# Scaling the second branch's rows in the middle stages of a hybrid trunk kernel, and starting its output pairs in text order

## The chip, the core and the metric

The kernel runs on one core of a Trainium2 chip. A core has TensorE (matmuls, "PE" in the profile; its weight loads are "PEld"), VectorE ("DVE"), ScalarE ("ACT"), GpSimd ("POOL") and SyncE ("SP"), each with a queue of its own that is worked off in order, and 16 DMA engines that all queues share. The metric is the device time of one execution in microseconds; several executions are made, and the median is given.

## What is computed

One layer of a decoder trunk on a sequence of 1024 tokens with 1024 channels, float32. Two branches (HGRN2 and GLA, both gated linear attention) run on the same normalised input; each is normalised, gated, projected, and the two are merged by sigmoid gates:

```python
proj = h @ w_in[l]
hq, hf, hi, hz, gq, gk, gv, gz, ga, mg = jnp.split(proj, IN_OFFSETS, axis=-1)
y_h = hgrn2_branch(hq, hf, hi, hz, lb_all[l], hgrn_norm_w[l])
y_g = gla_branch(gq, gk, gv, gz, ga, gla_alpha_w[l], gla_alpha_b[l], gla_norm_w[l])
u_h = y_h @ w_branch[l, 0]
u_g = y_g @ w_branch[l, 1]
mg = jax.nn.sigmoid(mg.reshape(B, T, N_BRANCH, D_MODEL))
merged = mg[:, :, 0] * u_h + mg[:, :, 1] * u_g
x = x + gate[:, None, :] * (merged @ w_out[l])
return rms_norm(x, final_norm_w)
```

The part that matters here is the end of the HGRN2 branch. Its norm runs over all 1024 channels, so its factor for a token is known only when the last of its eight heads is done:

```python
o = rms_norm(o.reshape(B, T, HGRN_WIDTH), norm_w)
return o * jax.nn.silu(hz)
```

## The kernel before

**Tiles.** Work tiles come from a pool of 46 slots of 128 partitions x 1024 float32 (`Slots`). A slot that is freed goes to the end of a list, and the next request takes the one at its head; a tile may therefore have to wait for the last use of the tile that had the slot before. Every float32 matmul of size is made of three: operands are split into a high part (cast by ACT, L195, L1297, L1319) and a low part (the difference, by VectorE, L196, L1298, L1320), and high x high, high x low and low x high are added up.

**First part, up to about 816 us.** Projections of the input run as jobs of a `Stream`, one after another, their matmuls on L518, L577 to L579, L620 to L622. Between them `Stream.weave` puts small pieces of two tracks: `side`, the attention heads (generators that yield after each piece how many units of matmul work to wait for), and `back`, preparations such as sums of weights. One unit passes with each piece of a job. The products with the silu gate close each job (L929 on ACT, L930 on VectorE).

**Second part, `last_stages`, from about 816 us on.** Four stages b = 0 to 3 of 1024 x 1024 x 1024 products: the merge gates of the GLA and of the HGRN2 branch (b = 0, 1), then the projection of the GLA branch (b = 2) and of the HGRN2 branch (b = 3). Each is made with seven products of half size in place of eight, in the order `PRODUCTS = (1, 2, 5, 3, 6, 7, 4)`. Each product has four pairs i = 0 to 3; `Pair.run(p)` issues 12 matmuls of 128x128 by 128x512 (L1377), with one unit of weave after the sixth and one after the twelfth, so two units for a pair. So (0, 5, 3) is stage 0, product 5, pair 3. `Pair.after` takes sums and snapshots of the accumulators (L1349, L1351, L1364). The last head of HGRN2 still runs on the side track in stage 0; the other side work and the whole back track are through by then.

The left operands are prepared ahead in `prep_duo` (L1319 on ACT, L1320 on VectorE, one for two pairs). The right operands of stages 2 and 3 are the four quadrants of a branch's output. They are read from memory by `load_quad` (L1269), two tiles each, in the stage before; `combine` (L1280) takes differences of them and `build` (L1297, L1298) splits them.

**The factor.** After head 7 of HGRN2, `inverse_root` computes 1/rms for each token (L940 to L943) and the tile is kept in `rst_h` until stage 3 begins. `scale_quad` (L1276) multiplies the quadrants of `yh` with it when they have been loaded, at the end of stage 2. All of `yh` was stored by `put_act` (L893, POOL's queue).

**Queues and order.** Loads are issued on SP's queue, stores of intermediates on POOL's. Outside a first stretch with a fixed order, the order of the instructions on each engine is made when the kernel is built: a planner runs the program text on a model of the engines and lets an instruction that it takes to be ready go ahead of earlier ones on the same engine that it takes to be waiting. `tc.keep_in_program_order(m)` binds an instruction behind the one that stands before it on its engine in the text. Slots are handed out in text order, whatever the planner does.

**Accumulators.** Pairs 0 and 1 of (0, 1) share one tile of two banks, pairs 2 and 3 another. One of the two is free when stage 0 begins, the other is the one that the last job's product (L930) still reads.

Of the kernel before, what the change touches and what calls it, by code (L numbers as in the profile page):

```python
# [15 lines left out]
P = 128  # L16
# [66 lines left out]
def hybrid_trunk_kernel(  # L83
# [6 lines left out]
    nc = tc.nc  # L90
# [9 lines left out]
    S = Slots(sp, N_SLOTS)  # L100
# [71 lines left out]
    h_d, yg_d, yh_d = acts("h"), acts("yg"), acts("yh")  # L172
# [889 lines left out]
    def hgrn_attention(h):  # L1062
        st = h_state
        y = [None]
        sq = [None]

        def post(vh, half, po):
            if half == 0:
                y[0], sq[0] = st.pop(("z", h)), S.get([T])
            sl = slice(half * 512, half * 512 + 512)  # L1070
            nc.scalar.activation(sq[0][:, sl], po, AF.Square)
            nc.vector.scalar_tensor_tensor(y[0][:, sl], po, vec[:, R_HN + h:R_HN + h + 1],
                                           y[0][:, sl], ALU.mult, ALU.mult)

        yield from attention(st.pop(("q", h)), st.pop(("k", h)), st.pop(("f", h)), lambda: st[("v", h // 4)],
                             h % 4 * P, P, post)
        if h % 4 == 3:
            S.free(*st.pop(("v", h // 4)))
        put_act(yh_d, h, y[0])
        if ssq[0] is None:  # L1080
            ssq[0] = sq[0]
        else:
            nc.gpsimd.tensor_add(ssq[0], ssq[0], sq[0])
            S.free(sq[0])
        if h == 7:
            yield 2
            rst = S.get([T])
            inverse_root(rst, ssq[0], D)
            S.free(ssq[0])
            rst_h[0] = rst  # L1090

    def hgrn_v(h):
        def done(v):
# [174 lines left out]
        for kk in range(2):  # L1268
            nc.sync.dma_start(quads[b, z][kk], part_of(acts_of[b], int(z[0]) - 1, int(z[1]) - 1, kk))  # L1269

    def scale_quad(b, z):
        half = int(z[1]) - 1
        rst = rst_h[0][:, half * 512:half * 512 + 512].unsqueeze(1).to_broadcast([P, 2, 512])
        for t in quads[b, z]:
            v = t.rearrange("p (a t) -> p a t", a=2)
            nc.vector.tensor_mul(v, v, rst)  # L1276

    def combine(b, dst, x, y):
        for kk in range(2):
            nc.vector.tensor_sub(quads[b, dst][kk], quads[b, x][kk], quads[b, y][kk])  # L1280
# [60 lines left out]
    class Pair:  # L1341
# [25 lines left out]
        def run(self, p):  # L1367
            if p in (1, 5):
                self.bank[BANK[p]] = R.get()
            o = self.bank[BANK[p]]  # L1370
            hi, lo = (z[:, self.i % 2, :] for z in wt[self.b, p, self.i // 2])
            h = H[0 if self.b == 1 else self.b, p]
            for kt in range(4):
                h_hi, h_lo = (z[kt // 2][:, kt % 2, :] for z in h)
                sl = slice(kt * P, (kt + 1) * P)
                for n, (a, c) in enumerate(((hi, h_hi), (hi, h_lo), (lo, h_hi))):
                    nc.tensor.matmul(o, a[:, sl], c, start=(p in (1, 5) and kt == 0 and n == 0),  # L1377
                                     stop=(kt == 3 and n == 2), skip_group_check=True)
                if kt % 2:
                    stream.weave(1)  # L1380
            if self.i % 2:
                S.free(*wt.pop((self.b, p, self.i // 2)))
# [153 lines left out]
    for b in (2, 3):  # L1536
        for p, i, z in ((3, 3, "11"), (6, 1, "21"), (6, 3, "12"), (7, 2, "22")):
            after(b - 1, p, i, lambda b=b, z=z: load_quad(b, z))
            if b == 3:
                p, i = {(3, 3): (7, 2), (6, 1): (7, 3), (6, 3): (4, 2), (7, 2): (4, 3)}[p, i]  # L1540
                after(2, p, i, lambda z=z: scale_quad(3, z))
        after(b, 1, 2, lambda b=b: combine(b, "11", "12", "11"))
        after(b, 2, 2, lambda b=b: combine(b, "12", "12", "22"))

# [6 lines left out]
            combine(b, "21", "21", "22")  # L1551
            drop_quad(b, "22")
        after(b, 6, 2, last_of_all)
    after(3, 1, 0, lambda: S.free(rst_h[0]))

    def begin():
        fetch_factor(GROUPS[0])
# [47 lines left out]
```

## Time and profile before

| | |
|---|---|
| median of 3 runs | 1246.13 us (1244.64 to 1246.9) |
| profiled execution | 1243.66 us, of which span 1242.0 us |
| mean granted TensorE clock | 0.993 |
| bytes moved by DMA | 168.82 MB |

The times in the profile are those of one execution, from its first to its last instruction. A row of a timeline shows the start in us, the duration in us, the engine, the line of the kernel, the operation, what it writes and reads (tile names without their numbers; `b` is any tile of the 46 slots, `pd`, `pm` and `sc_ps` are accumulators), its shapes and, in brackets, the idle time of the engine before it and what ended it. A row of a table of windows shows for a stretch how long each engine was busy and with how many instructions, the granted clock, the share of time in which the DMA engines were busy and the GB/s that they moved.

### The profile page before, as it was taken

How to read it: one execution, taken by the hardware profiler on the slowest of the kernel's cores; microseconds unless marked ns; L12 is line 12 of the kernel's file. 1: busy time of each engine (PE TensorE's matmuls, PEld its weight loads, DVE VectorE, ACT ScalarE, POOL GpSimd, SP SyncE). 2: the span in 40 equal slices, each digit the busy share in tenths (PEclk: the TensorE clock that was granted, in tenths of full speed). 3: DMA queues.
4: the chain of work that ended last, by engine and by line, in shares of the span. 5: the costliest groups of instructions: out<-in, count | busy, mean ns of one | idle time of the engine just before them, and what ended most of it. 6: DMA issues, size and time to landing. Idle time of an engine off the chain costs nothing.

```text
span 1242.0 us, 20840 instructions
## 1 busy us (share of the span) xinstructions
PE 1202.8 (97%) x8627; PEld 996.6 (80%) x8627; DVE 759.9 (61%) x1225; ACT 535.3 (43%) x786; POOL 115.7 (9%) x201
## 2 busy tenths in 40 slices
PE   5999999999999999999999999999999999998997
PEld 3676889889798888788887878877888887787786
DVE  5635535584848466877774366785422758979443
ACT  5547643434434234334323324457643644454222
POOL 4100000202111121011110101011100000000000
PEclk9989999999999999999999999999999999999999
DMA  9714010744544267265251112244547456235202
GB/s 325 258 52 136 24 28 19 260 157 145 170 151 147 81 200 244 96 187 166 74 186 52 51 35 69 75 156 169 184 158 243 154 186 195 77 102 178 110 35 101
DMA packets 126928, 168.82 MB, mean 136 GB/s; under 512 B 7019, under 2 KB 97185, under 8 KB 126834
## 3 DMA queue, kind: packets, MB, share of 16 engines
q1 hardware_dynamic: 115234, 129.53, 33.4%
q0 software_dynamic: 11552, 37.97, 8.0%
q8 instruction: 67, 1.10, 0.4%
q14 instruction: 27, 0.22, 0.1%
q10 hardware_dynamic: 48, 0.01, 0.0%
HBM read 125.53 MB, written 41.94 MB: 135 GB/s over the span
## 4 chain that ended last, share of the span: by engine, by line
PE 59%; issue 23%; DVE 8%; DMA 4%; ACT 3%; POOL 2%; SPq 0%; POOLq 0%; DVEq 0%; ACTq 0%
PE pd L518 14%; PE pd L1377 9%; PE sc_ps L1377 5%; PE pm L1377 4%; PE pd L343 3%; PE pd L620 2%; PE pd L621 2%; PE pd L622 2%; PE sc_ps L343 1%; DVE b L196 1%; PE pm L825 1%; PE pd L1147 1%; PE pd L1148 1%; PE pd L1149 1%; DMA b<-yh 1%
## 5 line engine op out<-in xcount | busy, mean ns | idle before, releaser
L518 PE MATMUL pd<-b,b 128*128 128x512 f32 x1632 | 386.7, 393 | 0.0
L518 PEld LDWEIGHTS pd<-b,b 128*128 128x128 f32 x1632 | 302.4, 188 | 64.3 <-issue 0.7
L1377 PE MATMUL pd<-b,b 128*128 128x512 f32 x720 | 175.5, 395 | 3.0 <-DVE b L930 1.5
L1377 PEld LDWEIGHTS pd<-b,b 128*128 128x128 f32 x720 | 134.4, 189 | 35.7 <-DVE b L930 1.9
L196 DVE TENSOR_TENSOR b<-b,b 128x1024 fp32r<-128x1024 f32 (+2 forms) x99 | 102.5, 1045 | 92.0 <-ACT b L195 75.3
L195 ACT CAST b<-b 128x1024 fp32r<-128x1024 f32 (+2 forms) x99 | 86.7, 888 | 109.1 <-PE pd L518 16.9
L1320 DVE TENSOR_TENSOR b<-b,b 128x1024 fp32r<-128x1024 f32 x56 | 68.2, 1222 | 68.8 <-ACT b L1319 50.5
L1319 ACT CAST b<-b 128x1024 fp32r<-128x1024 f32 x56 | 58.4, 1050 | 65.3 <-PE pd L1377 19.1
L1377 PE MATMUL sc_ps<-b,b 128*128 128x512 f32 x324 | 79.0, 391 | 0.9 <-ACT scT L770 0.9
L1377 PE MATMUL pm<-b,b 128*128 128x512 f32 x300 | 72.7, 390 | 3.3 <-DVE b L1320 3.3
L577 PE MATMUL pd<-b,b 128*128 128x256 f32 x256 | 74.6, 291 | 0.0
L579 PE MATMUL pd<-b,b 128*128 128x256 f32 x256 | 72.5, 283 | 0.0
L578 PE MATMUL pd<-b,b 128*128 128x256 f32 x256 | 72.4, 283 | 0.0
L1377 PEld LDWEIGHTS sc_ps<-b,b 128*128 128x128 f32 x324 | 60.4, 188 | 14.2 <-ACT scT L770 1.4
L1377 PEld LDWEIGHTS pm<-b,b 128*128 128x128 f32 x300 | 56.6, 189 | 15.6 <-DVE b L1320 3.7
L343 PE MATMUL pd<-b,b 128*128 128x512 f32 x192 | 56.6, 431 | 4.8 <-DVE b L322 2.6
L1298 DVE TENSOR_TENSOR b<-b,b 128x1024 fp32r<-128x1024 f32 x36 | 45.1, 1262 | 18.1 <-ACT b L1297 10.3
L1235 POOL DMA_DIRECT2D ws<-b x64 | 34.6, 541 | 192.6 <-DVE b L1229 87.3
L620 PE MATMUL pd<-b,b 128*128 128x512 f32 x128 | 51.3, 401 | 0.0
L343 PEld LDWEIGHTS pd<-b,b 128*128 128x128 f32 x192 | 37.3, 203 | 17.2 <-issue 3.4
L712 ACT COPY xb<-b 128x512 f32<-128x512 f32 x48 | 29.4, 620 | 48.8 <-PE sc_ps L692 26.6
L621 PE MATMUL pd<-b,b 128*128 128x512 f32 x128 | 50.0, 390 | 0.0
(269 smaller groups left out, 2010.6 us busy)
## 6 DMA issues: line engine op xcount, KB each, us to landing
b<-in_w_in_dram SPq DMA_DIRECT2D x66, 512.0 KB, 4.1
ws<-b POOLq DMA_DIRECT2D x64, 256.0 KB, 3.4
b<-ws SPq DMA_DIRECT2D x32, 512.0 KB, 4.4
b<-in_x_dram SPq DMA_DIRECT2D x16, 512.0 KB, 5.6
b<-in_ada_w_dram SPq DMA_DIRECT2D x32, 256.0 KB, 6.5
b<-in_w_branch_dram SPq DMA_DIRECT2D x16, 512.0 KB, 4.4
b<-h SPq DMA_DIRECT2D x14, 512.0 KB, 4.0
b<-in_w_in_dram SPq DMA_DIRECT2D x24, 256.0 KB, 3.8
```

Source lines behind the costliest of these rows:

```text
L195: nc.scalar.copy(hi, src)
L196: nc.vector.tensor_sub(lo, src, hi.bitcast(F32))
L343: nc.tensor.matmul(accs[f], wg(a, d, f), b[d][:, half * 512:half * 512 + 512], start=(d == 0 and n == 0), stop=(d == KT - 1 and n == 2))
L518: nc.tensor.matmul(ps[0:w, th * 512:(th + 1) * 512], a[:, k, 0:w], b[:, th * 512:(th + 1) * 512], start=(k == 0 and n == 0), stop=(k == KT ...
L577: nc.tensor.matmul(o, lh, hi[:, k % 4, :], start=(k == 0), stop=False)
L578: nc.tensor.matmul(o, lh, lo[:, k % 4, :], start=False, stop=False)
L579: nc.tensor.matmul(o, ll, hi[:, k % 4, :], start=False, stop=(k == KT - 1))
L620: nc.tensor.matmul(o, lh, hi[:, k % 2, :], start=(k == 0), stop=False)
L621: nc.tensor.matmul(o, lh, lo[:, k % 2, :], start=False, stop=False)
L1319: nc.scalar.copy(hi, t)
L1320: nc.vector.tensor_sub(lo, t, hi.bitcast(F32))
L1377: nc.tensor.matmul(o, a[:, sl], c, start=(p in (1, 5) and kt == 0 and n == 0), stop=(kt == 3 and n == 2), skip_group_check=True)
```

## The change

Three edits. A generator `scale_rows` goes onto the back track when the factor has been computed: it loads each of the eight tiles of `yh`, multiplies it with the factor, and stores it back to where it came from. `scale_quad` and its four calls at the end of stage 2 are gone, and the factor's slot is freed when the eight tiles are done, not after (3, 1, 0). And the first matmul of each of the four pairs of (0, 1) is bound to its place in the text.

```diff
             inverse_root(rst, ssq[0], D)
             S.free(ssq[0])
             rst_h[0] = rst
+            stream.back.append([scale_rows(), 1])
+
+    def scale_rows():
+
+        for half in range(2):
+            rst = rst_h[0][:, half * 512:half * 512 + 512].unsqueeze(1).to_broadcast([P, 2, 512])
+            for i in range(4):
+                y = S.get([2, 512])
+                nc.sync.dma_start(y.rearrange("p a t -> p (a t)"), yh_d[half][i])
+                yield 4
+                nc.vector.tensor_mul(y, y, rst)
+                nc.gpsimd.dma_start(yh_d[half][i], y.rearrange("p a t -> p (a t)"))
+                S.free(y)
+                yield 2
+        S.free(rst_h[0])
...
-    def scale_quad(b, z):
-        half = int(z[1]) - 1
-        rst = rst_h[0][:, half * 512:half * 512 + 512].unsqueeze(1).to_broadcast([P, 2, 512])
-        for t in quads[b, z]:
-            v = t.rearrange("p (a t) -> p a t", a=2)
-            nc.vector.tensor_mul(v, v, rst)
...
-                    nc.tensor.matmul(o, a[:, sl], c, start=(p in (1, 5) and kt == 0 and n == 0),
-                                     stop=(kt == 3 and n == 2), skip_group_check=True)
+                    m = nc.tensor.matmul(o, a[:, sl], c, start=(p in (1, 5) and kt == 0 and n == 0),
+                                         stop=(kt == 3 and n == 2), skip_group_check=True)
+                    if (self.b, p, kt, n) == (0, 1, 0, 0):
+                        tc.keep_in_program_order(m)
...
-            if b == 3:
-                p, i = {(3, 3): (7, 2), (6, 1): (7, 3), (6, 3): (4, 2), (7, 2): (4, 3)}[p, i]
-                after(2, p, i, lambda z=z: scale_quad(3, z))
...
-    after(3, 1, 0, lambda: S.free(rst_h[0]))
```

## The prediction

> **What bounds the kernel now.** I read the page first, then TensorE's timeline from the start of the closing stages to their end, then VectorE's timeline and the table of windows over the same stretch, then the waits of single lines.
>
> ```profile
> span 1242.0 us, 20840 instructions
> PE 1202.8 (97%) x8627; PEld 996.6 (80%) x8627; DVE 759.9 (61%) x1225; ACT 535.3 (43%) x786; POOL 115.7 (9%) x201
> ...
> 900.00:1040.00 140.00, 140.00 (x619) 115.79 (x618) 1.00 0.57 182
> 1040.00:1100.00 60.00, 58.98 (x255) 46.93 (x254) 1.00 0.42 130
> 1132.00:1146.20 14.20, 10.50 (x37) 7.56 (x35) 0.88 0.42 146
> ```
>
> TensorE is busy for 97% of the span, so every change has to show up as fewer or more empty microseconds on TensorE. The last three rows are windows of the closing-stage matmuls (L1377) alone; the number in brackets is their count. From 900 to 1040 us, 619 of them take 140 us, 0.226 us each, with nothing lost. From 1040 to 1100 us only 255 fit in 60 us: 60 − 255 × 0.226 = 2.3 us lost. From 1132 to 1146.2 it is 14.2 − 37 × 0.226 = 5.8 us, less about 0.4 us for two matmuls of the output projection that stand between them: 5.4 us. These two places, and the opening of the closing stages at 816 to 850 us, are where time can be had.
>
> ```profile
> 870.00:900.00 30.00, 30.00 (x133) 24.40 (x132) 14.78 (x16) 19.12 (x25) 3.78 (x7) 1.00 0.57 178
> 900.00:930.00 30.00, 30.00 (x134) 24.70 (x133) 8.49 (x7) 11.99 (x18) 2.69 (x5) 1.00 0.48 158
> 1020.00:1050.00 30.00, 29.37 (x130) 24.03 (x129) 22.44 (x25) 10.18 (x12) 0.00 (x0) 1.00 0.67 211
> 1050.00:1080.00 30.00, 29.87 (x130) 23.74 (x129) 29.53 (x32) 14.29 (x16) 0.00 (x0) 1.00 0.39 119
> 1080.00:1110.00 30.00, 29.73 (x131) 24.02 (x130) 22.55 (x23) 15.21 (x18) 0.00 (x0) 1.00 0.28 87
> 1110.00:1140.00 30.00, 26.59 (x113) 21.08 (x113) 29.05 (x43) 16.85 (x23) 0.00 (x0) 0.98 0.33 107
> ```
>
> The columns are PE, PEld, DVE, ACT, POOL busy, the granted clock, the DMA engines' share, GB/s. VectorE is full from 1050 to 1080 us (29.53 of 30) and again from 1110 to 1140 (29.05); from 870 to 930 us it is half empty or emptier.
>
> **Part 1: eight multiplies leave the end of stage b = 2.**
>
> ```profile
> L1276 DVE TENSOR_TENSOR b<-b,b x8: 1212/1216/1224, 1020.6 to 1061.7; 128x1024 f32<-128x1024 f32 x8
>   DMA b<-yh: 7.5, 3
> ...
> 1041.38 1.22 DVE L1276 TENSOR_TENSOR b<-b,b 128x1024 f32<-128x1024 f32 x1 [0.99 <-DMA b<-yh]
> 1044.86 0.68 DVE L1364 TENSOR_TENSOR b<-pd,b 128x512 f32<-128x512 f32 x1
> ...
> 1045.69 3.00 PE L1377 MATMUL pd<-b,b 128*128 128x512 f32 x12 [0.63 <-DVE b L1364]
> 1088.10 0.93 PE L1377 MATMUL pd<-b,b 128*128 128x512 f32 x3 [0.27 <-ACT b L1319]
> ```
>
> The multiplies hold VectorE for 8 × 1.216 = 9.7 us, and three of them made the queue stand 7.5 us in all until their rows had landed. Right behind one such wait, TensorE waits for the sum of L1364 (0.63 us), and it goes on losing fractions until 1100 us. Without 17 us of work and waiting, VectorE's jam of 1050 to 1080 us is gone, and with it most of the 2.3 us. Bounds: a gain of 2.3 us at most, since no more is lost there; 0 at least, if the interleaving of the pairs at the start of b = 3 costs it anyway. I take three quarters, 1.7 us, because the largest piece hangs on VectorE by its own row. The quads' loads stay where they are, so no queue changes here.
>
> **Part 2: the same eight multiplies, with a load and a store each, enter the middle stages.** The generator starts with the last unit of pair (0, 5, 3) and yields 6 units for a row; a pair gives 2 units and takes 12 × 0.226 = 2.7 us. So a row comes every 3 pairs, 8.1 us, and eight rows take 65 us, from about 867 to 933 us. The factor is there in time:
>
> ```profile
> 870.93 1.06 ACT L943 ACTIVATE b<-b 128x1024 f32<-128x1024 f32 x1
> L893 POOL DMA_DIRECT2D yh<-b x16: 539/548/556, 489.4 to 862.6; - x16
> fx<-b POOLq DMA_DIRECT2D x8, 512.0 KB, 6.6
> b<-yh SPq DMA_DIRECT2D x8, 512.0 KB, 3.4
> L1269 SPq DMA_DIRECT2D b<-yh x8: 319/338/426, 1016.3 to 1046.7; - x8
> ```
>
> VectorE gets 8 × 1.22 us over 65 us, 15% more on a load of 49% (14.78 of 30) and then 28%. POOL gets 8 issues of 0.55 us, 4.4 us, and is nearly idle. SP gets 8 issues of 0.34 us. A row lands in 3.4 us, is scaled in 1.2 and stored in 6.6 (as f_x's 512 KB were), so a slot is out for some 12 us. The DMA engines move 8 × 2 × 512 KB = 8.4 MB more in 65 us, 129 GB/s, on top of 178 and 158 GB/s; the stretch of 1020 to 1050 us carried 211 at a share of 0.67, so the share goes up to about 0.9, and landings may take longer. All of this lies under TensorE as long as VectorE's preparations stay ahead of it. The tightest one is this:
>
> ```profile
> 885.52 1.22 DVE L1320 TENSOR_TENSOR b<-b,b 128x1024 fp32r<-128x1024 f32 x1
> ...
> 889.52 1.98 PE L1377 MATMUL pm<-b,b 128*128 128x512 f32 x8
> ...
> 904.41 1.23 DVE L1320 TENSOR_TENSOR b<-b,b 128x1024 fp32r<-128x1024 f32 x1 [5.58 <-DMA gate<-b]
> SPq L1312 <- DVE b L1320: 17.0, 2, 10.5
> ```
>
> The low part made at 885.52 is done at 886.74, and the third matmul of the group that begins at 889.52 reads it, at 889.97: 3.2 us to spare; the neighbours have more. A multiply before it costs 1.2 us of that, and TensorE notices nothing. One that stands in VectorE's queue for its row as long as the worst of L1276 (3 waits share 7.5 us, so about 3.5 us for the longest) costs 3.5 + 1.2 − 3.2 = 1.5 us. Behind the waiting multiply stand the L1320 splits and the sums of L1364, and for them wait TensorE and SP, whose next weight load needs the slot that L1320 frees. Bounds: 0, and the price of rival 1. I take 0.5 us, a third of one such hit. The row holds one slot of 46 and the factor's slot comes back two stages earlier; after (3, 1, 0) the slots follow one another as before.
>
> **Part 3: the four pairs of (0, 1) begin in text order.**
>
> ```profile
> 816.27 1.52 PE L1377 MATMUL pd<-b,b 128*128 128x512 f32 x6
> 817.72 1.31 PE L660 MATMUL sc_ps<-xb,b 128*32 128x80 f32 x64
> 818.96 1.65 PE L1377 MATMUL pd<-b,b 128*128 128x512 f32 x6
> 822.10 5.73 PE L1377 MATMUL pd<-b,b 128*128 128x512 f32 x24 [1.48 <-DVE b L930]
> ...
> 820.83 1.21 DVE L930 TENSOR_TENSOR b<-b,pd 128x1024 f32<-128x1024 f32 x1
> 821.55 0.59 ACT L1351 ACTIVATE b<-pd 128x512 f32<-128x512 f32 x1
> ```
>
> In the order that the planner made of the old kernel, pair 0 comes first (the two sixes), then four matmuls of pair 2, all of pair 1, the rest of pair 2, and pair 3. Pair 2 waits for the bank that L930 reads until 822.04: that is the 1.48 us. Text order puts pair 1 in front. But its first matmul waits, by the old program's semaphores, for the snapshot of pair 0 (L1351; both lie in one accumulator tile), which ends at 822.14. One wait takes the place of the other, 0.1 us later. Bounds: −1.6 us, if ACT's queue is planned otherwise and the snapshot comes at once; +2.7 us, one pair's time, if pair 2 then waits again. I take +0.2 us.
>
> **Sum.** −1.7 + 0.5 + 0.2 = −1.0 us. The profiled execution took 1243.66 us (span 1242.0 and 1.66 around it), so 1242.7; it lies 2.47 us below the median of 1246.13, so the median of the new kernel comes to 1245.1 us.
>
> **Rivals.** 1. *Slower: the row loads get stuck in SP's queue, and VectorE stands behind them.* SP is in order, and in this very stretch it stood 10.5 us for one slot (the last row of the fence on preparations). A row's load behind such a wait comes up to 10.5 us late; its multiply, planned for a row on time, then holds VectorE, and beyond the 3.2 us to spare TensorE loses up to 7.3 us. It decides from a delay of 3.2 us on. At half of that, 10.5/2 + 1.2 − 3.2 = 3.3, and twice over the eight rows, 6.6: with −1.7 and +0.2 that is +5.1, so 1251.2 us; in one place only, +1.8. For it: three of eight rows were late when loaded with less traffic. Against it: the planner places a multiply behind the load it knows of, and SP's wait was itself for an L1320.
>
> 2. *Much faster: the stall at the end goes too.*
>
> ```profile
> 1126.90 1.05 ACT L1319 CAST b<-b 128x1024 fp32r<-128x1024 f32 x1 [1.95 <-PE pd L1377]
> 1135.51 1.22 DVE L1320 TENSOR_TENSOR b<-b,b 128x1024 fp32r<-128x1024 f32 x1
> ...
> 1136.78 0.50 PE L1377 MATMUL pm<-b,b 128*128 128x512 f32 x1 [3.31 <-DVE b L1320]
> 1137.38 4.49 PE L1377 MATMUL pd<-b,b 128*128 128x512 f32 x12
> ```
>
> The cast of the last weights ends at 1127.95, yet their low part is made 7.6 us later, behind the sums of the pairs before. TensorE waits 3.31 us, and the 12 matmuls after it take 4.49 us where 12 took 2.88 before; the granted clock of this window is 0.88. If the planner, freed of eight multiplies, moves that split up by 3.5 us, all of the 5.4 us go: 1246.13 − 5.4 − 1.0 = 1239.7. Against it: VectorE idled between 1080 and 1110 us (22.55 of 30), so the second jam does not inherit the first. The Trainium skill (TensorE: Matmul & The Clock Gate, "What's actually happening") says that the clock falls to half after an idle window of about 3.4 us and comes back after a busy one. The trace agrees in the 3.31 us gap and the 0.88. By that rule a split only a little earlier would save the slow matmuls at once and a new gap of that length anywhere would cost some 2 us on top of itself; without it the end stall is worth 3.3 us alone.
>
> 3. *Nothing is gained:* b = 3 interleaves its pairs as before, the 2.3 us stay, and the change costs nothing either: 1246.1. For it: the largest single wait there is 0.63 us.
>
> 4. *Text order costs a pair* (part 3's upper bound): 1246.13 + 2.7 − 1.7 + 0.5 = 1247.6, or more if the later pairs shift as well.
>
> **How the numbers follow.** Forecast 40%, rival 1 28%, rival 2 22%, rival 3 5%, rival 4 5%. The measurement of this kernel tells about 0.2% (2.5 us) from no change. The forecast's own range is 1242.5 to 1246.5; with the other places of the closing stages falling well it passes −2.5 us in 16 of its 40 parts. Faster by over 0.2%: 16 + 22 = 38%. Slower: 25 of rival 1 and all 5 of rival 4, 30%. Within: 24 + 3 + 5 = 32%. The range runs from 1238.5 (both stalls gone with the 1.6 us of part 3's lower bound in part) to 1251.2 (rival 1).
>
> **What would show it.** Part 1: no multiply of the rows between 1020 and 1062 us, VectorE well under 29 of 30 us from 1050 to 1080, and close to 265 closing matmuls in the 60 us that held 255. Part 2: eight multiplies of about 1.22 us from 870 to 935 us, and no TensorE wait there; a wait of VectorE for yh over 3 us followed by a TensorE wait for L1320 speaks for rival 1. Part 3: one wait of about 1.5 us near 822 us, now for ACT's snapshot. The end: the wait of 3.3 us and the slow matmuls after it stay. The prediction is wrong if TensorE loses time in the middle stages, or if the order at the end of b = 3 changes.

## The result and the profile after

The changed kernel takes 1249.93 us (median of 17 runs, 1246.96 to 1252.88), the kernel before in the same session 1244.0 us (17 runs, 1241.44 to 1249.43): a ratio of 1.0044, with a 95% interval of 1.0032 to 1.0056, so 5.5 us slower by the ratio (the two medians lie 5.9 us apart) where 1.0 us faster was forecast. The profiled execution took 1250.22 us, with a span of 1248.5 us where the span before was 1242.0.

Where the 6.5 us of span lie is read by counting the matmuls of the closing stages, 48 for a product, in both traces (L1377 before, L1385 after; the lines after L1090 have moved by 8 to 15, L1364 to L1372, L1320 to L1328, L1319 to L1327, L1351 to L1359, and the multiply is L1101). A product's time is from its first matmul to the next product's first.

| stretch, us | before | after | |
|---|---|---|---|
| (0,5) | 16.07 | 17.34 | +1.27 |
| (0,3) | 12.60 | 11.38 | −1.22 |
| **(0,7)** | **11.13** | **16.95** | **+5.82** |
| (2,7), (2,4), (3,1), (3,2), (3,5) together | 56.99 | 56.03 | −0.96 |
| (3,4) to its last matmul | 16.73 | 17.88 | +1.15 |

The rest is small: −0.3 ahead of the closing stages, within 0.4 in the other products, and +0.85 behind the last one. (0,5) and (0,3) cancel; hold_slots below, which only shifts the slots, has the same +1.27 and −1.22. The +1.15 of (3,4) comes from the clock. The wait there is of the same length in both kernels (3.31 and 3.41 us), but behind it the granted clock was half for 3.4 us before and for 6.8 us after, as these windows of before and of after show (columns PE, PEld, DVE, ACT, POOL, granted clock, DMA share, GB/s):

```profile
1138.58:1142.00 3.42, 3.42 (x9) 2.65 (x9) 3.42 (x4) 0.60 (x1) 0.00 (x0) 0.50 0.50 180
```

```profile
1140.37:1147.20 6.83, 5.33 (x12) 4.05 (x13) 6.83 (x9) 1.42 (x3) 0.00 (x0) 0.50 0.33 88
```

hold_slots and mul_bound, which scale the rows at the end of stage 2 as before, also have 6.8 us at half clock there, so this part does not need the change.

The windows of the page's engines say the same as the table. First all of the kernel after (the same columns), then its closing matmuls alone:

```profile
870.00:900.00 30.00, 26.36 (x107) 20.59 (x106) 17.84 (x18) 17.29 (x23) 4.84 (x9) 0.94 0.85 277
1050.00:1080.00 30.00, 30.00 (x134) 24.61 (x133) 25.14 (x28) 13.24 (x15) 0.00 (x0) 1.00 0.36 107
```

```profile
1040.00:1100.00 60.00, 59.06 (x259) 47.91 (x258) 1.00 0.39 123
```

From 1050 to 1080 us TensorE now loses nothing and VectorE is at 25.14 of 30 us in place of 29.53, as forecast. The loss is from 870 to 900 us: 107 matmuls where 133 fitted. There the timelines of TensorE, VectorE and ScalarE after show this:

```profile
886.44 2.88 PE L1385 MATMUL pd<-b,b 128*128 128x512 f32 x12
890.25 0.73 PE L1385 MATMUL pm<-b,b 128*128 128x512 f32 x2 [0.93 <-ACT b L1327]
891.51 0.97 PE L1385 MATMUL pm<-b,b 128*128 128x512 f32 x3 [0.53 <-DVE b L1328]
894.67 4.57 PE L1385 MATMUL pd<-b,b 128*128 128x512 f32 x12 [2.18 <-DVE b L1372]
```

```profile
872.99 2.36 DVE L1101 TENSOR_TENSOR b<-b,b 128x1024 f32<-128x1024 f32 x2 [4.69 <-ACT b L943]
...
882.50 1.23 DVE L1101 TENSOR_TENSOR b<-b,b 128x1024 f32<-128x1024 f32 x1 [3.75 <-DMA b<-yh]
883.65 0.68 DVE L1372 TENSOR_TENSOR b<-b,sc_ps 128x512 f32<-128x512 f32 x1
...
893.93 0.68 DVE L1372 TENSOR_TENSOR b<-pd,b 128x512 f32<-128x512 f32 x1
```

```profile
884.36 0.63 ACT L1457 ACTIVATE b<-b 128x512 f32<-128x512 f32 x1 [4.07 <-DVE b L1372]
...
889.15 2.00 ACT L1327 CAST b<-b 128x1024 fp32r<-128x1024 f32 x2 [1.72 <-issue]
```

```profile
885.28 0.55 POOL L1458 DMA_DIRECT2D gate<-b  x1 [0.73 <-ACT b L1457]
```

And the same places of the kernel before, VectorE and TensorE:

```profile
879.38 0.69 DVE L1364 TENSOR_TENSOR b<-b,sc_ps 128x512 f32<-128x512 f32 x1 [4.16 <-ACT b L1351]
...
890.71 0.68 DVE L1364 TENSOR_TENSOR b<-pd,b 128x512 f32<-128x512 f32 x1
```

```profile
891.45 3.02 PE L1377 MATMUL pd<-b,b 128*128 128x512 f32 x12
```

Read from top to bottom: the multiply of the third row holds VectorE for 3.75 us, because the row has not landed, and is done at about 883.7. The first sum of product 6, which came at 879.38 before, is queued behind it and comes at 883.65. ScalarE's sigmoid of that sum (L1457) has waited 4.07 us for it, GpSimd's store of the gate follows at 885.28. By the program's semaphores the slot of that stored tile is the one that was given to the high part of the second weights of product 7; its cast (L1327) starts at 889.15, 3.9 us after the store was issued and 0.06 us after it landed. TensorE waits 0.93 us for it, then 0.53 for its low part, then 2.18 for the sum at 893.93, which reads the accumulator that the next matmuls add to. Then the 12 matmuls that took 3.02 us before take 4.57, 1.55 more. These four make 5.2 of the 5.82 us.

The last two rows of before hold what the forecast overlooked. The sum at 890.71 ends at 891.39, and the 12 matmuls that need its accumulator begin at 891.45, **0.06 us** behind it. That is no slack at all: where TensorE plainly waits for this sum, the matmuls begin just as shortly behind its end (894.61 and 894.67 after, 893.53 and 893.59 in hold_slots). The forecast counted 3.2 us on VectorE in this very place.

Why was the third row late? SP's queue after, its waits (in total, times, longest), and the waits of the multiplies:

```profile
867.95 0.42 SPq L1320 DMA_DIRECT2D b<-in_w_in_dram  x1
876.51 0.32 SPq L1279 DMA_DIRECT2D b<-fx  x1
877.43 0.32 SPq L1099 DMA_DIRECT2D b<-yh  x1
```

```profile
SPq L1279 <- DVE b L1328: 8.0, 1, 8.0
SPq L1099 <- DMA yh<-b: 6.3, 2, 5.7
```

```profile
  DMA b<-yh: 15.8, 5
```

The last row is what VectorE's multiplies (L1101) waited for. SP stood 8.0 us at an f_x load whose slot a split on VectorE had not yet freed; the row's load behind it went out at 877.43 and landed 5 us later. That f_x load was hardly later than before (876.51 and 875.80): the row's load was put behind a wait that had been there already. All eight multiplies together stood 15.8 us for rows, in 5 places; the forecast's pattern was 7.5 us in 3. The longest of these waits, 6.24 us, is not the one that cost time. It lies in stage 1, whose products take 10.88 us each, as before (VectorE's timeline after):

```profile
928.77 1.23 DVE L1101 TENSOR_TENSOR b<-b,b 128x1024 f32<-128x1024 f32 x1 [6.24 <-DMA b<-yh]
```

### The profile page after: what moved, and what is told of

Same layout as the page of the kernel before. It is cut to its first block, busy times and chain, and to the rows that moved or that the text cites. A ratio compares the mean times of both kernels' runs of the same rounds, so it can differ in the third digit from the quotient of the medians.

```text
span 1248.5 us, 20896 instructions
## 1 busy us (share of the span) xinstructions
PE 1203.7 (96%) x8627; PEld 997.3 (80%) x8627; DVE 759.8 (61%) x1225; ACT 534.6 (43%) x786; POOL 120.0 (10%) x209
## 4 chain that ended last, share of the span: by engine, by line
PE 67%; issue 15%; DVE 5%; DMA 3%; ACT 3%; POOL 1%; POOLq 0%; SPq 0%; DVEq 0%; ACTq 0%
PE pd L518 20%; PE pd L1385 11%; PE sc_ps L1385 5%; PE pm L1385 4%; PE pd L620 2%; PE pd L621 2%; PE pd L622 2%; PE pm L825 2%; PE pm L827 1%; PE pm L806 1%; PE pd L343 1%; PE pd L1162 1%; PE pd L1163 1%; PE pd L1164 1%; DMA b<-in_w_branch_dram 1%
## 5 line engine op out<-in xcount | busy, mean ns | idle before, releaser
L518 PE MATMUL pd<-b,b 128*128 128x512 f32 x1632 | 386.8, 393 | 0.0
L518 PEld LDWEIGHTS pd<-b,b 128*128 128x128 f32 x1632 | 302.4, 188 | 64.4 <-issue 0.7
L1385 PE MATMUL pd<-b,b 128*128 128x512 f32 x720 | 177.0, 398 | 5.2 <-DVE b L1372 2.2
L1385 PEld LDWEIGHTS pd<-b,b 128*128 128x128 f32 x720 | 136.7, 192 | 37.0 <-DVE b L1372 2.6
L1328 DVE TENSOR_TENSOR b<-b,b 128x1024 fp32r<-128x1024 f32 x56 | 69.4, 1249 | 63.1 <-ACT b L1327 31.0
L1327 ACT CAST b<-b 128x1024 fp32r<-128x1024 f32 x56 | 58.2, 1049 | 67.1 <-PE pd L1385 21.0
L1385 PE MATMUL sc_ps<-b,b 128*128 128x512 f32 x324 | 79.2, 391 | 0.7 <-ACT scT L770 0.7
L1385 PE MATMUL pm<-b,b 128*128 128x512 f32 x300 | 73.3, 392 | 5.1 <-DVE b L1328 3.9
L1385 PEld LDWEIGHTS sc_ps<-b,b 128*128 128x128 f32 x324 | 60.4, 188 | 13.9 <-ACT scT L770 1.1
L1385 PEld LDWEIGHTS pm<-b,b 128*128 128x128 f32 x300 | 56.2, 188 | 18.3 <-DVE b L1328 4.8
L343 PE MATMUL pd<-b,b 128*128 128x512 f32 x192 | 54.5, 418 | 4.8 <-DVE b L322 2.6
L1305 ACT CAST b<-b 128x1024 fp32r<-128x1024 f32 x36 | 37.6, 1050 | 35.0 <-DMA b<-fx 6.3
L620 PE MATMUL pd<-b,b 128*128 128x512 f32 x128 | 52.0, 407 | 0.0
L621 PE MATMUL pd<-b,b 128*128 128x512 f32 x128 | 50.5, 394 | 0.0
L622 PE MATMUL pd<-b,b 128*128 128x512 f32 x128 | 50.4, 393 | 0.0
```

The lines of the kernel that those rows point to most:

```text
L343: nc.tensor.matmul(accs[f], wg(a, d, f), b[d][:, half * 512:half * 512 + 512], start=(d == 0 and n == 0), stop=(d == KT - 1 and n == 2))
L518: nc.tensor.matmul(ps[0:w, th * 512:(th + 1) * 512], a[:, k, 0:w], b[:, th * 512:(th + 1) * 512], start=(k == 0 and n == 0), stop=(k == KT ...
L620: nc.tensor.matmul(o, lh, hi[:, k % 2, :], start=(k == 0), stop=False)
L621: nc.tensor.matmul(o, lh, lo[:, k % 2, :], start=False, stop=False)
L622: nc.tensor.matmul(o, ll, hi[:, k % 2, :], start=False, stop=(k == KT - 1))
L1328: nc.vector.tensor_sub(lo, t, hi.bitcast(F32))
```

## The experiments

Each ratio is against runs of the kernel before on the same chip, with its 95% interval; 0.1% is 1.24 us. The times of products are those of one profiled execution.

### The parts of the change alone

**order_only**: the kernel before, with the binding of the first matmuls of (0,1).

```diff
+                    if (self.b, p, kt, n) == (0, 1, 0, 0):
+                        tc.keep_in_program_order(m)
```

> The old kernel with the binding of the four first matmuls alone. Theory 1 (the rows' multiplies, standing in VectorE's queue around product 7 of stage 0, cost the time): within 1 us of the kernel before, one TensorE wait of about 1.5 to 1.8 us near 820 us as in both kernels, no wait near 890 us. Theory 2 (the order of the pairs shifts the later instructions into the stall): at least 3 us slower, with a stall near 890 us and half-clock matmuls behind it.

0.9994 [0.998, 1.0008], as theory 1 says. Part 3 is worth nothing that can be measured (+0.2 us was forecast). In TensorE's timeline of the changed kernel the wait of 1.48 us for L930 has become one for the snapshot.

```profile
821.96 5.74 PE L1385 MATMUL pd<-b,b 128*128 128x512 f32 x24 [1.64 <-ACT b L1359]
```

**rows_only**: the changed kernel without that binding.

```diff
-                    if (self.b, p, kt, n) == (0, 1, 0, 0):
-                        tc.keep_in_program_order(m)
```

> The changed kernel without the binding: rows scaled in the middle, pairs free to float. Theory 1: 4.5 to 6.5 us slower than the kernel before, with the stall in product 7 of stage 0. Theory 2: within 1.5 us of the kernel before.

1.0043 [1.0029, 1.0058]: the whole loss, as theory 1 says. (0,7) takes 15.81 us, but (0,5) 18.88, so it is spread in another way.

**no_scale**: the kernel before without the eight multiplies at the end of stage 2, so that the rows stay unscaled.

```diff
-            if b == 3:
-                p, i = {(3, 3): (7, 2), (6, 1): (7, 3), (6, 3): (4, 2), (7, 2): (4, 3)}[p, i]
-                after(2, p, i, lambda z=z: scale_quad(3, z))
```

> The old kernel without the eight multiplies at the end of stage 2; the second branch's rows are not scaled at all. It shows the most that taking them out of the closing stages can bring. My prediction: 1.7 us faster, 2.3 at most. The trace of the changed kernel, which lost 1.65 us between 1070 and 1100 us where the old one lost 2.6 between 1040 and 1100, says about 1 us faster. If the jam of VectorE is the cost, 2.3 us or more.

0.9992 [0.9978, 1.0007], which can't be told from no change. In the traces the five products of the border take 56.14 us in place of 56.99. So Part 1 is 0.85 us here and 0.96 in the changed kernel, not 1.7. What takes part of it back stands in (3,5), in TensorE's timelines of before and after:

```profile
1088.10 0.93 PE L1377 MATMUL pd<-b,b 128*128 128x512 f32 x3 [0.27 <-ACT b L1319]
```

```profile
1092.62 0.93 PE L1385 MATMUL pd<-b,b 128*128 128x512 f32 x3 [0.94 <-ACT b L1327]
```

The wait for a cast grows from 0.27 to 0.94 us, and (3,5) from 11.49 to 12.16.

### What of the rows costs

**hold_slots**: the kernel before; a generator takes and returns the slots as the rows do, with a one-column memset on GpSimd, no load, multiply or store.

```diff
+        for i in range(8):
+            y = S.get([2, 512])
+            nc.gpsimd.memset(y[:, 0, 0:1], 0.0)
+            yield 4
+            S.free(y)
+            yield 2
```

> The old kernel, rows still scaled at the end of stage 2, in which eight times one slot of the 46 is taken out of the list and given back, in the rhythm of the rows (a 128x1 clearing on POOL is all that is done with it). Theory A (the shift of the slots alone makes the stall: the high part of the second weights of product 7 gets a slot whose gate store is late): a TensorE stall of 3 us or more in product 7 of stage 0, 3 us or more slower. Theory B (VectorE standing for its row alone): within 1 us of before. Theory C (both together: the shift ties that cast to the store of the first gate, and the late multiply makes the sum, so the gate and its store, 4 us late): under 1.5 us slower.

1.002 [1.0007, 1.0033], 2.5 us, between the three theories: the shift of the slots has a price of its own, (0,7) takes 13.51 us. TensorE waits for the same sum again, but the clock stays. The sum stands behind a split (L1307) that waited 1.65 us (TensorE's timeline, then VectorE's):

```profile
893.59 3.06 PE L1386 MATMUL pd<-b,b 128*128 128x512 f32 x12 [2.29 <-DVE b L1373]
```

```profile
891.71 1.23 DVE L1307 TENSOR_TENSOR b<-b,b 128x1024 fp32r<-128x1024 f32 x1 [1.65 <-ACT b L1456]
892.85 0.68 DVE L1373 TENSOR_TENSOR b<-pd,b 128x512 f32<-128x512 f32 x1
```

**rows_in_xb**: the changed kernel with the rows in a scratch tile that always lies there, so no slot is taken.

```diff
-                y = S.get([2, 512])
+                y = xb_f[:, i % 2 * 1024:i % 2 * 1024 + 1024].rearrange("p (a t) -> p a t", a=2)
```

> The changed kernel with the rows in two parts of xb, the attention's scratch tile, which is idle by then: no slot is taken, all else stays. Theory A: the stall in product 7 is gone, about 1 us faster than before. Theory B: the stall stays, 4 us or more slower. Theory C: most of it is gone, between 1 us faster and 1.5 us slower.

1.0054 [1.0041, 1.0067], (0,7) 17.11 us. Without any slot the loss is as large, so slots are not needed for it. Its VectorE stands for rows in the same way:

```profile
880.99 1.22 DVE L1101 TENSOR_TENSOR xb<-xb,b 128x1024 f32<-128x1024 f32 x1 [4.41 <-DMA xb<-yh]
882.13 0.68 DVE L1371 TENSOR_TENSOR b<-b,sc_ps 128x512 f32<-128x512 f32 x1
```

**rows_no_mul**: the changed kernel without the multiply; the rows go through a slot and back as they are.

```diff
-                nc.vector.tensor_mul(y, y, rst)
```

> The changed kernel without the eight multiplies (the rows go to a slot and back unscaled): slots, SP, POOL and DMA traffic as in the changed kernel, nothing of it on VectorE. Theory A: the stall stays, 4 us or more slower than before. Theories B and C: no stall of over 1.5 us in product 7, and at most 1 us slower than before, rather faster.

1.0091 [1.0075, 1.0108], yet (0,7) takes 11.08 us: the stall is gone with the multiplies. The time is lost elsewhere, in (0,5), 24.02 us in place of 16.07. Freed of the multiplies, the plan has two of the rows' loads from 840.69 us on (one, at 838.99, in the changed kernel). Behind them SP stands 5.5 us more at a load of weights, and the f_x load that follows goes out at 853.70, 3.0 us later than in the changed kernel, counted from the start of the closing stages. ScalarE's cast stands 5.26 us for it, and behind that cast the last head's squares and the sum for the factor come late. TensorE waits 4.50 us for the cast of that sum (the row names a split of VectorE that ended at the same moment), and the granted clock is half for 6.8 us. How much of this the second row's load causes is not shown. ScalarE's timeline, then TensorE's:

```profile
859.43 1.05 ACT L1304 CAST b<-b 128x1024 fp32r<-128x1024 f32 x1 [5.26 <-DMA b<-fx]
```

```profile
866.50 1.22 PE L940 MATMUL pm<-b,ones_r 128*128 128x512 f32 x2 [4.50 <-DVE b L1327]
```

**rows_xb_ahead**: the rows in the scratch tile, each loaded a row ahead, 9 units before its multiply.

```diff
+            yield 3
+            if r < 7:
+                nc.sync.dma_start(y[(r + 1) % 2], yh_d[(r + 1) // 4][(r + 1) % 4])
+            yield 3
```

> As the rows in xb, with each row loaded nine units (12 us) ahead of its multiply in place of four (5.4 us), so that VectorE does not stand for a row. Theories B and C: no stall in product 7, 0.5 to 1.5 us faster than the kernel before, the gain of the closing stages alone. If 1.2 us of multiply every 8 us is too much for VectorE there by itself: slower by 1 us or more, with TensorE waiting for low parts.

1.0064 [1.005, 1.0078], no cure: no theory foresaw that the plan floats the multiplies forward as well. The longest wait for a row is 4.71 us, and (0,7) and (0,4) take 14.63 and 14.75 us.

**mul_only**: the kernel before with eight extra multiplies of the scratch tile, nothing loaded or stored.

```diff
+            yield 4
+            v = xb_f[:, i % 2 * 1024:i % 2 * 1024 + 1024].rearrange("p (a t) -> p a t", a=2)
+            nc.vector.tensor_mul(v, v, rst)
+            yield 2
```

> The kernel before, with eight extra multiplies of 128x1024 on VectorE at the places in the text where the changed kernel has its own; they work on a scratch tile that always lies there, so there is no load, no store, no slot, and nothing to wait for. The rows are still scaled at the end of stage 2. Theory W (what costs is VectorE standing for rows that are late): the multiplies alone cost what their 1.22 us find too little room, 0 to 1.2 us in all, with no TensorE wait over 1.3 us between 880 and 905 us. Theory O (the eight multiplies' own 9.7 us on VectorE are what does not fit): product 7 of stage 0 takes 13 us or more in place of 11.1, and the run is 2 us or more slower than before.

1.0027 [1.0013, 1.004], (0,7) 14.69 us: this looked like theory O. But with nothing to wait for, the plan put five of the eight in a row, ahead of the first sum of product 6 (VectorE's timeline, then TensorE's):

```profile
879.30 5.76 DVE L1099 TENSOR_TENSOR xb<-xb,b 128x1024 f32<-128x1024 f32 x5
884.98 0.68 DVE L1374 TENSOR_TENSOR b<-b,sc_ps 128x512 f32<-128x512 f32 x1
```

```profile
895.25 4.62 PE L1387 MATMUL pd<-b,b 128*128 128x512 f32 x12 [1.91 <-DVE b L1374]
```

**mul_bound**: the same eight, each bound to its place in the text.

```diff
-            nc.vector.tensor_mul(v, v, rst)
+            tc.keep_in_program_order(nc.vector.tensor_mul(v, v, rst))
```

> The kernel before with eight extra multiplies on a scratch tile as in mul_only, each now bound to its place in the text, so that they come one every three pairs and cannot crowd together; the rows are still scaled at the end of stage 2. One of them then stands just ahead of the sum that in the kernel before ended 0.06 us ahead of the matmul that needs it. Theory S (the sums of product 7 have no slack, so even one multiply ahead of them shows): product 7 takes 12.0 us or more in place of 11.1, TensorE waiting for that sum for about 1.2 us, and the run is 1 to 2.5 us slower than before. Rival (it was the crowding of seven multiplies within 8 us that cost in mul_only): product 7 takes at most 11.3 us, and the run is within 0.7 us of before.

1.0001 [0.9988, 1.0014], (0,7) 10.97 us. The rival holds: spread out and with no row to wait for, the 9.7 us of VectorE cost nothing. (The first two stand 3.80 us for the factor, without harm.) One of them fell just behind the tight sum, not ahead of it, so that a single multiply ahead of it costs 1.2 us was not tried (VectorE's timeline):

```profile
879.48 0.69 DVE L1374 TENSOR_TENSOR b<-b,sc_ps 128x512 f32<-128x512 f32 x1 [2.75 <-ACT b L1361]
...
890.87 0.68 DVE L1374 TENSOR_TENSOR b<-pd,b 128x512 f32<-128x512 f32 x1
891.47 1.21 DVE L1099 TENSOR_TENSOR xb<-xb,b 128x1024 f32<-128x1024 f32 x1
```

**loads_only**: the kernel before with the eight loads into the scratch tile, not used.

```diff
+            nc.sync.dma_start(xb_f[:, i % 2 * 1024:i % 2 * 1024 + 1024], yh_d[i // 4][i % 4])
+            yield 6
```

> The kernel before, with the eight loads of the second branch's rows on SP's queue at the places where the changed kernel has them, into a scratch tile that always lies there; they are not multiplied and not stored, and the rows are still scaled at the end of stage 2. Theory Q (a row's load that waits, for the tile that the row was stored from or for its landing place, holds up the weight and factor loads behind it on SP's in-order queue): 2 us or more slower than before, with a TensorE wait for a cast or a split over 1 us in product 5, 7 or 4 of stage 0, and a wait of over 4 us of SP at a row's load. Rival W: the loads alone cost nothing, under 1 us, since nothing on VectorE stands for them.

1.0011 [1.0, 1.0022], between the two expectations. SP did stand for the rows (13.6 us in 4 waits, the longest 4.2), and product 6 lost 1.06 us to a late copy of ScalarE; (0,7) took 11.08.

**rows_pool**: the changed kernel with the rows multiplied on GpSimd.

```diff
-                nc.vector.tensor_mul(y, y, rst)
+                nc.gpsimd.tensor_mul(y, y, rst)
```

> The changed kernel with the eight multiplies on GpSimd in place of VectorE: the rows are loaded, scaled and stored at the same places, in the same slots. Theory W: VectorE no longer stands for rows, so the sum behind which TensorE waited 2.18 us in product 7 of stage 0 comes in time; what is left are the price of the shifted slots (about 2 us) and the gain of about 1 us at the border of stages 2 and 3: 0.5 to 1.5 us slower than before. Theory O' (slots and SP's queue carry the loss, VectorE's waits little): 4 us or more slower than before, as the changed kernel is.

1.0089 [1.0069, 1.0108], and (0,7) 20.60 us: the size is that of theory O', but neither expectation had the way. The multiply stands in another queue, that of the gate stores (GpSimd's timeline, then TensorE's):

```profile
889.04 2.39 POOL L1101 TENSOR_TENSOR b<-b,b 128x1024 f32<-128x1024 f32 x1 [7.64 <-DMA b<-yh]
891.73 0.59 POOL L1102 DMA_DIRECT2D yh<-b  x1 [0.30 <-POOL b L1101]
892.32 1.08 POOL L1458 DMA_DIRECT2D gate<-b  x2
```

```profile
896.94 2.48 PE L1385 MATMUL pm<-b,b 128*128 128x512 f32 x4 [4.96 <-ACT b L1327]
```

This shows the lower half of the chain by itself: VectorE never stands for a row, but the gate store is late, and the cast that TensorE waits for runs at 895.85, 3.5 us after the store's issue and 0.07 us after its landing. Another 4.45 us are lost in (1,5), 15.33 us.

### The rows at another place

**late_rows** and **late_pool**: the rows begin 36 units later, in stage 1, multiplied on VectorE and on GpSimd.

```diff
-            stream.back.append([scale_rows(), 1])
+            stream.back.append([scale_rows(), 37])
```

> The changed kernel with the rows beginning 36 units later, in product 1 of stage 1, where the weights' low parts are made 9 to 20 us ahead of use. Theory 1: the stall near 890 us is gone, TensorE waits nowhere in stage 1, and the kernel is 0.5 to 1.5 us faster than the one before (the gain at the end of stage 2 alone). If the rows cost time wherever they stand (DMA traffic, the in-order queues), it is still 3 us or more slower.

> The changed kernel with the rows begun 36 units later, in stage 1, and multiplied on GpSimd. Of the late start with VectorE two losses were left: 1.07 us in product 4 of stage 0 and 0.8 us in product 7 of stage 1, the latter behind a multiply that stood 4.65 us for its row. Theory W: the second goes, and the run is between 0 and 1 us faster or slower than before, product 7 of stage 1 at 11.2 us or less. Rival Q: the loss in product 7 of stage 1 stays (11.7 us or more), since it comes with the loads and not with the multiply.

1.0013 [1.0002, 1.0024] and 1.0003 [0.999, 1.0016]: late_rows is 1.6 us slower, between its two expectations, and late_pool is as theory W says. (0,7) is sound in both, 11.29 and 11.14 us, but (0,4) takes 12.05 and 12.79. TensorE's waits there (0.87 us, ended at 900.97, and 1.60 us, ended at 901.67) are for ScalarE and come ahead of the first row's load (905.73 and 906.63). So no load of a row is behind them; why ScalarE is late there is not shown. On VectorE a multiply stands 4.65 us for its row in (1,7), 11.93 us; on GpSimd that product takes 10.88.

**rows_pause**: two rows at their place, six after a pause of 40 units.

```diff
-                yield 2
+                yield 2 if (half, i) != (0, 1) else 40
```

> The changed kernel with a pause of 40 units behind the second row: two rows are scaled in products 3 and 6 of stage 0, none in product 7 or 4, and six from the middle of stage 1 on. Theory S (the loss is what stands ahead of the sums in products 7 and 4): product 7 takes 11.1 to 11.5 us in place of 16.95, and the run is 0 to 1 us faster than before or the same. Rival T (the two slots that the first rows take shift the later ones, or the early loads hold up SP's queue): product 7 or 4 of stage 0 still takes 12.5 us or more, and the run is 1.5 us or more slower than before.

1.0046 [1.0025, 1.0068]. (0,7) takes 11.63 us, (0,4) 10.97, near theory S; but the total is that of rival T, because (0,5) takes 20.26 us. There ScalarE's cast of weights stands 3.17 us for its load, and TensorE waits 1.97 us for the factor's cast behind it. The first row's load comes at the same place as in the changed kernel, so that load alone does not explain it; the cause is open. (0,1), ahead of every row, took 17.33 us: Part 3's wait for the snapshot is 2.00 us here, and the clock falls behind it, so that 24 matmuls take 7.38 us in place of 5.74.

```profile
822.20 7.38 PE L1385 MATMUL pd<-b,b 128*128 128x512 f32 x24 [2.00 <-ACT b L1359]
```

**later_rows** and **later_pool**: 50 units later.

> The changed kernel with the rows begun 50 units later, from the middle of stage 1 on, 14 units behind late_rows. Theory S: stage 0 is as before (product 7 at 11.1 us and product 4 at 11.0 in place of 12.05 in late_rows, since no row's load reaches back into it), the border of stages 2 and 3 gains about 1 us, and the run is 0.5 to 1.5 us faster than before. Rival L (a row's load goes ahead of its place whatever it is given, and VectorE stands for it): product 7 or 4 of some stage loses 0.8 us or more, and the run is not faster than before.

> As later_rows, with the multiplies on GpSimd. Theory S: as fast as later_rows within 0.5 us where VectorE does not stand for a row there; faster than it by the TensorE waits of stage 1 where it does. Rival: slower than later_rows by 1 us or more, with a TensorE wait for a cast behind a store that is queued behind a multiply on GpSimd, as in rows_pool.

1.0001 [0.999, 1.0013] and 1.0027 [1.0015, 1.0039]. With VectorE, stage 0 is as before ((0,7) 11.17, (0,4) 10.97), the border takes 56.03 us, and the multiplies stand 25.0 us for rows without any loss in stage 1, where the sums have room. The 0.96 us gained are given back in small pieces: (0,1) +0.34, (2,2) +0.44, (2,5) +0.14, the last product +0.39. So a place without cost exists, as theory S says, but it gains nothing that can be measured. On GpSimd (0,1) and (2,2) lost 2.1 and 1.9 us; in (0,1), ahead of every row, it is Part 3's wait again (1.94 us, and 24 matmuls in 7.37).

### The stall at the end

**end_pool**: the kernel before, with the last of the L1320 splits on GpSimd. **later_end**: the same in later_rows.

```diff
-        nc.vector.tensor_sub(lo, t, hi.bitcast(F32))
+        (nc.gpsimd if duo == DUOS[-1] else nc.vector).tensor_sub(lo, t, hi.bitcast(F32))
```

> The kernel before, with the low part of the last weights (the one split for which TensorE stood 3.31 us at 1136.78) made by GpSimd, which has nothing to do there. The cast before it ends at 1127.95; a tile of this size takes GpSimd 2.4 us, so it would be ready at about 1130.5, ahead of the matmuls of 1133. Theory E (the end stall is that split's place behind the sums on VectorE and nothing else): wait and slow matmuls both go, 5.4 us less by the trace, 4 to 5.5 us faster than before. Rival (the sums behind which the split stood, or the tile that they read, hold TensorE next): less than 2 us faster, with a new TensorE wait for a sum of VectorE near 1137 us.

> As later_rows (the whole change, with the rows begun 50 units later), with the low part of the last weights on GpSimd as in end_pool. Theory S: the rows cost nothing where they now are, so this is as fast as end_pool or up to 1 us faster. Rival (the gain at the border of stages 2 and 3 is taken back by small waits elsewhere, as in later_rows): the same as end_pool within 0.5 us.

0.9972 [0.9961, 0.9982] and 0.9977 [0.9968, 0.9986], 3.5 and 2.9 us faster than before: **both beat both kernels**, end_pool without any of the change. The 3.31 us wait and the slow matmuls are gone, (3,4) is 4.30 us shorter, and two smaller waits have come, the second in the output projection (end_pool's TensorE, GpSimd and VectorE):

```profile
1131.95 2.92 PE L1377 MATMUL pd<-b,b 128*128 128x512 f32 x12
1135.76 5.03 PE L1377 MATMUL pm<-b,b 128*128 128x512 f32 x21 [0.90 <-DVE b L1364]
...
1163.62 0.50 PE L1147 MATMUL pd<-b,b 128*128 128x512 f32 x1 [1.62 <-DVE xb L1152]
```

```profile
1131.45 2.42 POOL L1320 TENSOR_TENSOR b<-b,b 128x1024 fp32r<-128x1024 f32 x1 [215.07 <-DMA b<-in_final_norm_w_dram]
```

```profile
1130.43 0.69 DVE L196 TENSOR_TENSOR b<-b,b 128x512 fp32r<-128x512 f32 x1
...
1131.92 2.50 DVE L196 TENSOR_TENSOR b<-b,b 128x512 fp32r<-128x512 f32 x1 [0.19 <-ACT b L195]
```

A split of that size on VectorE takes 0.69 us; beside GpSimd's it took 2.50, and the sum behind it came late. The result lies between the two expectations. Later_end is not faster than end_pool: its rival holds.

## Why the prediction was wrong, point by point

**The step that failed is Part 2's cover**, "3.2 us to spare; the neighbours have more". It was taken from the L1320 split at 885.52 alone. The sums share VectorE's queue, and one of them had none, with TensorE 0.06 us behind its end; and a late sum has a second way to TensorE, over sigmoid, gate store, slot and cast. The wait of the multiply that did it was near the forecast, 3.75 us for 3.5 (the longest, 6.24 us, cost nothing). That step priced such a hit at 1.5 us; it took 5.8, and with it the term of Part 2, put at 0.5 us, was about 5.8. "The factor is there in time" was wrong too: the first two multiplies stood 4.69 us for it; mul_bound, with 3.80 us of the same wait, shows no loss.

What goes with the loss is how early the sums of product 6 come. The table gives how long ahead of the first matmul of (0,7) its first and its third sum start, in us, from the records of VectorE's sums and of the closing matmuls:

| kernel | first sum ahead | third sum ahead | time of (0,7) |
|---|---|---|---|
| before | 7.42 | 1.89 | 11.13 |
| mul_bound | 7.42 | 1.89 | 10.97 |
| late_rows | 7.42 | 1.89 | 11.29 |
| rows_pause | 7.45 | 1.88 | 11.63 |
| rows_no_mul | 7.42 | 1.63 | 11.08 |
| hold_slots | 7.42 | 0.54 | 13.51 |
| rows_xb_ahead | 4.31 | −0.49 | 14.63 |
| mul_only | 4.57 | −0.17 | 14.69 |
| rows_only | 4.73 | 0.78 | 15.81 |
| after | 2.80 | −1.14 | 16.95 |
| rows_in_xb | 4.61 | −0.24 | 17.11 |
| rows_pool | 6.61 | −3.34 | 20.60 |

In the other eight runs the third sum is 1.89 us ahead, and (0,7) takes 11.08 to 11.45 us. Where the third sum is 1.6 us ahead or more, (0,7) takes 11.63 us at most; where it is not, 13.5 or more, whatever made it late: a multiply that stands for its row (after, rows_only, rows_in_xb, rows_xb_ahead), multiplies in a heap (mul_only), the shift of the slots (hold_slots), a cast that stood 4.84 us for f_x (rows_pool, beside its late store). The third sum is a sign and not by itself the cause: in hold_slots TensorE waits for a later one. The same multiplies spread and without a row to wait for (mul_bound) cost nothing. So "TensorE notices nothing" was right of the work, spread out, and wrong of the wait.

**Part 1** was the right mechanism in the wrong size: VectorE's jam went, but the term was 0.85 to 0.96 us for 1.7 in the traces, because a cast is late next in (3,5). **Part 3** was right in the wait, and its 0.2 us fit the changed kernel (1.64 us for 1.48); in the runs with this binding the wait is 0.72 to 2.19 us. **Rival 1** named the mechanism that came, a load behind a slot wait on SP and VectorE behind the load, and its +5.1 us stands beside 5.5 measured; it was made up otherwise, of two hits of 3.3 us where there was one of 5.8. That its total came so near is in part luck. **Rival 2** did not come with this change: the wait in the last product is 3.41 us for 3.31. That it was one split's place in a queue is shown by end_pool, but 3.5 us were to be had and not 5.4.

Three things stay open. In hold_slots the shifted slots alone cost 2.5 us and in rows_no_mul, with the same shift, nothing in (0,7), so how much of the 5.8 us is the slots' share is not settled. What one multiply right ahead of the tight sum would cost was not measured. And the changed kernel with its multiplies bound to their places was not run: mul_bound takes away the rows and the planner's freedom at once, so it does not tell how much the binding alone would cure.

## What to carry to other kernels

When work is put into a stretch with idle time on an engine, look for the smallest slack among all instructions that share its queue, not for that of one kind, and follow what a late one holds up, through stores and the buffers they free. An instruction with a transfer to wait for costs its engine the wait as well as its work, and each queue that it is moved to (VectorE's, GpSimd's, SP's) has something else behind it: the same 1.2 us were free in mul_bound and went with a loss of 5.8 us in the changed kernel, where a wait of 6.24 us one stage later was free again. A planner that reorders will also move what is not bound, so that leaving a piece out (rows_no_mul, mul_only) can make another plan, and only the products' times tell which part of a total belongs to the edit.

## What the runs showed of the hardware

**The clock and the gap.** The length of a wait of TensorE does not say whether the clock falls: 12 matmuls behind 1.91 us took 4.62 us (mul_only, above), behind 2.29 us 3.06 (hold_slots, above), and in rows_xb_ahead behind 3.38 us 3.02:

```profile
898.38 3.02 PE L1387 MATMUL pd<-b,b 128*128 128x512 f32 x12 [3.38 <-DVE b L1374]
```

What says it is how the wait lies on a grid. In each of the 20 traces the changes of the granted clock are whole multiples of 3.413 us apart (but for the end of the record). Cut into windows of this grid from 780 us on, the traces have 27 windows at full clock in which TensorE's records leave 1.88 us or more idle, and a window at half clock follows each of them. It follows none of the 2168 that leave less than 1.70 us, and two of the six between (1.70 to 1.76 us). So about half a window idle was what it took. The 1.91 us of mul_only lie in one window (3.41 − 1.50), and the next has a clock of 0.50; the 3.38 us of rows_xb_ahead are split into 1.62 and 1.76 us, and the clock stays (columns as above, mul_only, then rows_xb_ahead):

```profile
891.93:895.34 3.41, 1.50 (x8) 0.93 (x6) 2.32 (x4) 1.21 (x3) 0.54 (x1) 1.00 1.10 369
895.34:898.76 3.42, 3.42 (x8) 2.66 (x9) 2.21 (x2) 0.52 (x1) 0.54 (x1) 0.50 0.57 195
```

```profile
893.20:896.62 3.42, 1.80 (x8) 1.14 (x7) 3.08 (x4) 0.77 (x2) 0.83 (x2) 1.00 0.77 265
896.62:900.03 3.41, 1.65 (x7) 1.39 (x8) 2.58 (x3) 0.63 (x1) 0.78 (x2) 1.00 0.97 326
```

The Trainium skill (TensorE: Matmul & The Clock Gate, "What's actually happening") says that the clock gate looks at free-running windows of about 3.4 us and throttles after an idle one. The grid agrees with free-running windows; that 1.91 us in a window was enough does not agree with a whole idle window, and there the measurement decides. In the changed kernel the fallen clock adds 4.57 − 3.02 = 1.55 us in the 12 matmuls behind the wait of 2.18 us.

**VectorE beside GpSimd.** VectorE's split of 2.50 us in end_pool ended at 1134.42, 0.55 us after GpSimd's at 1133.87; without GpSimd beside it, it takes 0.69. The Trainium skill (SBUF — State Buffer, "🔬 SBUF: two separate sides") says that an operation of VectorE with two SBUF inputs and one of GpSimd lock a pair of ports against each other for a whole instruction. The trace agrees: here work given to GpSimd at a tight place was paid for by VectorE.
